# Modulation sums shared by VectorE, ScalarE and GpSimd, and held back in two stages of a two-block transformer kernel

## The chip, the cores and the metric

The kernel runs on one core of one Trainium2 chip. A core has five engines that run their own instruction streams and wait for each other through semaphores: TensorE (matmuls, in the profile PE, its weight loads PEld), VectorE (DVE), ScalarE (ACT), GpSimd (POOL) and SyncE (SP), whose queue issues the DMAs here. The metric is the device time of one execution in microseconds; lower is better.

## What is computed

Two small diffusion-transformer blocks with two layers each work on 256 latent tokens and 256 context tokens of width 1024, all in float32. The part that the change touches is the modulation: for each of four layers two condition vectors (`c` for the latent tokens, `c_ctx` for the context) are multiplied by a matrix of 1024 x 6144, which gives six rows of scales, shifts and gates per condition.

```python
def _modulation(cond, w, b):
    m = jax.nn.silu(cond) @ w + b
    return jnp.split(m[:, None, :], 6, axis=-1)

# first block, per layer
ml = _modulation(c, ada_w[i], ada_b[i])
mc = _modulation(c_ctx[None, :], ada_w[i], ada_b[i])
hl = _modulate(x, ml[0], ml[1])
yl, yc = mixer(hl, hc, ...)          # layer 0: mLSTM, layer 1: MLA attention
x = _layer_norm(ALPHA * x + ml[2] * yl, ln_g[i, 0], ln_b[i, 0])
f = _conv_ffn(_modulate(x, ml[3], ml[4]), ...)
x = _layer_norm(ALPHA * x + ml[5] * f, ln_g[i, 1], ln_b[i, 1])
```

Layer 1 of each block keeps only the latent tokens after its mixer, so the later parts of its modulation are needed for one condition alone. The second block has the same modulation around a set of parallel mixers and an MLP.

## The kernel before

Activations lie transposed: 1024 features are eight tiles of 128 partitions, and the free dimension holds the 512 tokens (256 where only the latent ones are left). A projection takes a 128-column block of weights (512 KB) at a time. `weight` loads it into one of five `raw` buffers, ScalarE casts it to a rounded high part `wh` (L280), and the low part `wl`, raw minus high, is a subtraction (L281) of which every third goes to GpSimd and the others to VectorE. `mm3` then makes three matmuls per 128x128 tile (L286 to L288): high x high, high x low, low x high. A weight takes 24 matmuls, of 512 columns in the first layer and of 256 where only the latent half is worked on. The low parts of activations are VectorE's as well (L264).

The modulation is a generator, `ada`, that runs in the background. One step loads one 128x1024 piece of its matrix into a `raw` buffer and adds it, scaled by the condition's 128 values, to an accumulator of 128x1024 per condition: the first of eight steps is a scaling on ScalarE (L418), the other seven are one VectorE instruction each (L420). After the eighth step matmuls with a column of ones add up the partitions on TensorE (tile `pa`, L427), and small operations write the result to `mod` (L439). `ada(1)` and `ada(3)` use two conditions for their first two parts and one for the rest; `ada(0)`, of which four parts run in the background, and `ada(2)` use two everywhere.

`later` queues a generator with a rate; each `weight` calls `tick`, which adds the rate times the weight's size to a credit and makes one step for each whole credit. `finish` runs a generator to its end where its result is needed. So the steps lie between the weights of whatever stage follows: `ada(0)` over the mLSTM layer's `w_up`, `w_og`, gates and head projections, `ada(1)` and the start of `ada(2)` over the first FFN, the rest of `ada(2)` over the MLA layer and the start of the second FFN, `ada(3)` over the first MLP.

The order of all instructions on each engine is settled ahead of the run by a scheduler that works from priorities and its own estimate of times; on the chip each engine runs its list in that order. A norm ends each mixer and FFN: sums of the residual and its square on VectorE and GpSimd (L509, L513, L516), eleven small VectorE operations on 128x2 or 128x4 elements that depend on each other (L525, L343, L344, L322 to L328, L352), transposes on TensorE (L336), and then the normalised tiles (L921, L922).

## Time and profile before

| | |
|---|---|
| median of 3 runs | 2603.92 us (2596.65 to 2606.05) |
| profiled execution, its own time | 2603.71 us |
| span of the profile | 2601.8 us |
| TensorE busy | 2421.3 us, 93% |
| VectorE busy | 1660.9 us, 64% |
| ScalarE busy | 1128.3 us, 43% |
| GpSimd busy | 672.7 us, 26% |
| moved by DMA | 369.69 MB, mean 142 GB/s |

The profile is one execution, and its span is 1.9 us shorter than the time measured around it. Stages follow each other in the order of the program, so a window of the span is a stage: the mLSTM layer up to about 712 us, the first FFN to 1137, the MLA layer to 1365, the second FFN to 1595, then the second block. Busy shares of the whole span mix stages with different limits; the windows say more.

### The profile page before, as it was taken

Reading aid. Unit: us, or ns where it says so; the run is one execution under the profiler, and the core shown is the slowest. Engines: PE = TensorE matmul, PEld = TensorE weight load, DVE = VectorE, ACT = ScalarE, POOL = GpSimd, SP = SyncE. Lnnn points to the kernel's source line nnn. Section 1 sums busy time; section 2 is a strip of 40 time slices with the busy share of each in tenths; the row PEclk is TensorE's granted clock in tenths of the full one; section 3 lists DMA queues with packets and bytes.
Section 4 is the critical chain, followed back from the end, with each engine's and each line's share of the span. In section 5 each row is a group of like instructions: output and inputs, shape, how many; then the busy total and the mean of one; then the engine's idle time right before and its main releaser. Section 6 shows DMA issues by size and latency. Waiting matters only on the chain.

```text
span 2601.8 us, 36381 instructions
## 1 busy us (share of the span) xinstructions
PE 2421.3 (93%) x14038; PEld 2091.6 (80%) x14038; DVE 1660.9 (64%) x2656; ACT 1128.3 (43%) x1897; POOL 672.7 (26%) x449
## 2 busy tenths in 40 slices
PE   7998999999998999997885999978999999987998
PEld 5876888788897888886675899857888878977998
DVE  4866634433666755568888756797776555597665
ACT  4733334322434233335444445765533223475543
POOL 1111322312541111154023222261211112252222
PEclk9999999999998999998997999988999999997999
DMA  8565423433422555445344655121345545223553
GB/s 288 193 208 174 146 82 113 125 102 114 144 94 90 187 173 174 155 132 160 99 142 161 202 181 175 53 84 51 125 151 171 174 158 177 67 83 109 167 176 128
DMA packets 114749, 369.69 MB, mean 142 GB/s; under 512 B 12688, under 2 KB 17040, under 8 KB 114576
## 3 DMA queue, kind: packets, MB, share of 16 engines
q1 hardware_dynamic: 114576, 367.37, 43.5%
q8 instruction: 110, 1.80, 0.3%
q14 instruction: 63, 0.52, 0.1%
HBM read 357.88 MB, written 9.44 MB: 141 GB/s over the span
## 4 chain that ended last, share of the span: by engine, by line
PE 75%; DVE 13%; DMA 4%; ACT 3%; issue 3%; POOL 1%; SPq 0%; DVEq 0%; ACTq 0%; POOLq 0%
PE pm L286 20%; PE pm L288 20%; PE pm L287 20%; PE px L286 3%; PE px L287 3%; PE px L288 3%; DVE a L420 3%; DVE wl L281 2%; DMA raw<-in_ada 2%; DVE a L1408 1%; DVE a L264 1%; PE pa L427 1%; PE px L312 1%; ACT wh L280 1%; DVE a L281 1%
## 5 line engine op out<-in xcount | busy, mean ns | idle before, releaser
L286 PE MATMUL pm<-a,wh 128*128 128x512 f32 (+1 forms) x2432 | 844.5, 349 | 17.7 <-ACT wh L280 5.8
L288 PE MATMUL pm<-a,wl 128*128 128x512 f32 (+1 forms) x2432 | 840.2, 347 | 14.3 <-DVE wl L281 12.0
L287 PE MATMUL pm<-a,wh 128*128 128x512 f32 (+1 forms) x2432 | 841.8, 347 | 0.0
L280 ACT CAST wh<-raw 128x1024 fp32r<-128x1024 f32 (+2 forms) x421 | 420.3, 1001 | 749.0 <-PE pm L287 397.0
L281 POOL TENSOR_TENSOR wl<-raw,wh 128x1024 fp32r<-128x1024 f32 (+2 forms) x140 | 334.9, 2392 | 1432.1 <-ACT wh L280 1356.7
L286 PEld LDWEIGHTS pm<-a,wh 128*128 128x128 f32 x2432 | 468.6, 193 | 90.8 <-ACT wh L280 16.7
L288 PEld LDWEIGHTS pm<-a,wl 128*128 128x128 f32 x2432 | 468.2, 193 | 72.4 <-DVE wl L281 15.0
L287 PEld LDWEIGHTS pm<-a,wh 128*128 128x128 f32 x2432 | 469.7, 193 | 53.1 <-issue 1.6
L281 DVE TENSOR_TENSOR wl<-raw,wh 128x1024 fp32r<-128x1024 f32 (+2 forms) x281 | 345.3, 1231 | 199.1 <-ACT wh L280 197.3
L420 DVE SCALAR_TENSOR_TENSOR a<-raw,cs,a 128x1024 f32<-128x1024 f32 x252 | 365.0, 1471 | 140.4 <-DMA raw<-in_ada 137.6
L287 PE MATMUL pm<-a,a 128*128 128x256 f32 (+2 forms) x844 | 252.2, 301 | 10.6 <-DVE a L264 9.7
L286 PE MATMUL pm<-a,a 128*128 128x256 f32 (+2 forms) x844 | 248.6, 306 | 14.3 <-ACT a L280 3.6
L288 PE MATMUL pm<-a,a 128*128 128x256 f32 (+2 forms) x844 | 250.4, 300 | 1.9 <-DVE a L281 1.8
L286 PEld LDWEIGHTS pm<-a,a 128*128 128x128 f32 x844 | 167.3, 202 | 21.8 <-ACT a L263 5.6
L287 PEld LDWEIGHTS pm<-a,a 128*128 128x128 f32 x844 | 169.3, 201 | 15.3 <-DVE a L264 11.6
L288 PEld LDWEIGHTS pm<-a,a 128*128 128x128 f32 x844 | 168.9, 201 | 5.1 <-DVE a L281 2.9
L263 ACT CAST a<-t 128x256 fp32r<-128x256 f32 (+2 forms) x173 | 86.4, 507 | 158.9 <-DVE t L1712 96.7
L491 DVE SCALAR_TENSOR_TENSOR a<-pm,mod,a 128x256 f32<-128x256 f32 x188 | 87.0, 479 | 101.6 <-PE pm L288 101.1
L287 PE MATMUL pm<-wl,a 128*128 128x512 f32 (+1 forms) x336 | 131.1, 390 | 5.1 <-DVE wl L281 5.1
L264 DVE TENSOR_TENSOR a<-t,a 128x256 fp32r<-128x256 f32 (+2 forms) x173 | 110.0, 642 | 36.7 <-ACT a L263 34.6
L286 PE MATMUL pm<-wh,a 128*128 128x512 f32 (+1 forms) x336 | 129.1, 387 | 3.4 <-ACT a L263 3.4
L288 PE MATMUL pm<-wh,a 128*128 128x512 f32 (+1 forms) x336 | 128.4, 390 | 0.0
(308 smaller groups left out, 3416.3 us busy)
## 6 DMA issues: line engine op xcount, KB each, us to landing
raw<-in_ada SPq DMA_DIRECT2D x192, 512.0 KB, 4.2
raw<-in_w_m SPq DMA_DIRECT2D x128, 512.0 KB, 4.0
raw<-in_ffn_in SPq DMA_DIRECT2D x88, 512.0 KB, 4.1
raw<-in_w_qk SPq DMA_DIRECT2D x32, 512.0 KB, 3.6
raw<-in_w_v SPq DMA_DIRECT2D x32, 512.0 KB, 3.5
raw<-in_ffn_oa SPq DMA_DIRECT2D x32, 512.0 KB, 4.1
raw<-in_w_inb SPq DMA_DIRECT2D x28, 512.0 KB, 4.2
raw<-in_w_up SPq DMA_DIRECT2D x16, 512.0 KB, 4.8
```

The costliest lines, as they stand in the source:

```text
L263: self.nc.scalar.copy(hi, src)
L264: self.nc.vector.tensor_sub(lo, src, hi.bitcast(F32))
L280: nc.scalar.copy(hi, raw)
L281: eng.tensor_sub(lo, raw, hi.bitcast(F32))
L286: mm(out, ah, bh, start=start, stop=False)
L287: mm(out, ah, bl, start=False, stop=False)
L288: mm(out, al, bh, start=False, stop=stop)
L312: self.nc.tensor.matmul(out_ps[:, i * nt + t:i * nt + t + 1], a[:, c0 + t * P:c0 + (t + 1) * P], self.ones[:, 0:1], start=(k == 0), stop=( ...
L420: nc.vector.scalar_tensor_tensor(s, raw, c, s, op0=ALU.mult, op1=ALU.add)
L427: nc.tensor.matmul(ps[32 * i:32 * i + 32], self.ones[:, 0:32], acc[i // 2][:, 512 * (i % 2):512 * (i % 2) + 512], start=True, stop=True, t ...
L491: self.nc.vector.scalar_tensor_tensor(z[:, a:b], ps[:, a:b], gate[:, kt, w:w + 1], z[:, a:b], op0=ALU.mult, op1=ALU.add)
L1408: nc.vector.scalar_tensor_tensor(y3, x(i), w(i), y3, op0=ALU.mult, op1=ALU.add)
```

## The change

In a part with two conditions, the first condition's accumulator stays VectorE's. The second one's piece is scaled by ScalarE into a new tile, from the same pool of 31 tiles that holds activations, and GpSimd adds that tile to the accumulator. A part with one condition stays on VectorE. `pause` runs the steps of a part that has been begun to the part's end and then stops all steps until `hold` is reset; it is called ahead of the mLSTM heads and ahead of the MLA layer. The rates become 0.9 for `ada(0)` (from 0.8), 1.1 for `ada(1)` (from 0.8), 1.1 for `ada(2)` (from 1.2), and 0.6 for what is left of `ada(2)` after the MLA layer.

```diff
                     if kt == 0:
                         nc.scalar.activation(s, raw, AF.Copy, scale=c)
+                    elif s is acc[0]:
+                        nc.vector.scalar_tensor_tensor(s, raw, c, s, op0=ALU.mult, op1=ALU.add)
                     else:
-                        nc.vector.scalar_tensor_tensor(s, raw, c, s, op0=ALU.mult, op1=ALU.add)
+                        x = self.a4(F32, (P, D))
+                        nc.scalar.activation(x, raw, AF.Copy, scale=c)
+                        nc.gpsimd.tensor_add(s, s, x)
+                self.open = True
                 if kt < KD - 1:
                     yield
+            self.open = False
...
     def tick(self, size):
-        if not self.bg:
+        if not self.bg or self.hold:
             return
...
+    def pause(self):
+
+        while self.open:
+            next(self.bg[0][0])
+        self.hold = True
...
-    K.later(rest, 0.8)
+    K.later(rest, 0.9)
...
+    K.pause()
     qps = [qk_of(0)]
...
         y += head_out(hd, vp, pp)
+    K.hold = False
...
-        K.later(gen1, 0.8)
+        K.later(gen1, 1.1)
...
-        K.later(gen2, 1.2)
+        K.later(gen2, 1.1)
...
+        K.pause()
         _mla(K, h1, z, mod1, _Ln(K, z, g2, b2, K.affine(mod1, 4, 3, g2, b2), ALPHA, h, LAT, LAT))
+        K.hold = False
+        K.bg[0][1] = 0.6
```

In the program's order of loads, the first FFN has 54 modulation steps before and 72 after, the MLA layer 27 and none, the second FFN 15 and 24; the head projections have about ten before and none after, and `w_mo` gets 8.

VectorE at the norm that ends the MLA layer, before: `v` and `rs` are the norm's small tiles, the `a` tiles with `cs` the modulation's accumulators.

```order
L343 SCALAR_TENSOR_TENSOR v_10996<-st_10994 128x2
L420 SCALAR_TENSOR_TENSOR a_10957<-raw_11160,cs,a_10957 128x1024
L420 SCALAR_TENSOR_TENSOR a_10958<-raw_11160,cs,a_10958 128x1024
L344 SCALAR_TENSOR_TENSOR v_10996<-v_10996,st_10994 128x2
L420 SCALAR_TENSOR_TENSOR a_10957<-raw_11170,cs,a_10957 128x1024
L420 SCALAR_TENSOR_TENSOR a_10958<-raw_11170,cs,a_10958 128x1024
L322 TENSOR_SCALAR rs_10999<-v_10996 128x2
L420 SCALAR_TENSOR_TENSOR a_10957<-raw_11239,cs,a_10957 128x1024
L420 SCALAR_TENSOR_TENSOR a_10958<-raw_11239,cs,a_10958 128x1024
L323 TENSOR_TENSOR rs_10999<-rs_10999 128x2
```

The same place of the changed program, where the lines are numbered one and up to fifteen higher.

```order
L538 TENSOR_SCALAR st_11065<-px_11052 128x4
L344 SCALAR_TENSOR_TENSOR v_11067<-st_11065 128x2
L345 SCALAR_TENSOR_TENSOR v_11067<-v_11067,st_11065 128x2
L323 TENSOR_SCALAR rs_11070<-v_11067 128x2
L324 TENSOR_TENSOR rs_11070<-rs_11070 128x2
L325 SCALAR_TENSOR_TENSOR rs_11070<-rs_11070,v_11067 128x2
```

The modulation's accumulations are gone from between the norm's steps; they stand behind the norm in the changed order.

GpSimd at the first weights of the second FFN, before: the norm's last scalings (`ga`), then the low parts of every third weight.

```order
L927 TENSOR_SCALAR a_4945<-a_4945,ga_9193 128x256 x2
L281 TENSOR_TENSOR wl_11238<-raw_11235,wh_11237 128x1024
L281 TENSOR_TENSOR wl_11342<-raw_11339,wh_11341 128x1024
L281 TENSOR_TENSOR wl_11493<-raw_11490,wh_11492 128x1024
L281 TENSOR_TENSOR wl_11596<-raw_11593,wh_11595 128x1024
```

And in the changed program, where L425 is the new addition.

```order
L942 TENSOR_SCALAR a_4939<-a_4939,ga_9438 128x256 x2
L282 TENSOR_TENSOR wl_11301<-raw_11298,wh_11300 128x1024
L425 TENSOR_TENSOR a_11156<-a_11156,a_11234 128x1024
L425 TENSOR_TENSOR a_11156<-a_11156,a_11305 128x1024
L282 TENSOR_TENSOR wl_11389<-raw_11386,wh_11388 128x1024
L425 TENSOR_TENSOR a_11156<-a_11156,a_11381 128x1024
L425 TENSOR_TENSOR a_11156<-a_11156,a_11458 128x1024
L282 TENSOR_TENSOR wl_11536<-raw_11533,wh_11535 128x1024
```

Between two low parts of weights GpSimd now has one or two additions.

## Rows read from the trace of the kernel before

**Rows 1.** The page's first part: busy time by engine, share, instructions.

```profile
PE 2421.3 (93%) x14038; PEld 2091.6 (80%) x14038; DVE 1660.9 (64%) x2656; ACT 1128.3 (43%) x1897; POOL 672.7 (26%) x449
```

**Rows 2.** Windows by stage: length, busy time of each engine, clock, DMA share, GB/s.

```profile
257.00:405.00 148.00, 147.16 (x699) 122.11 (x699) 69.39 (x104) 54.70 (x102) 42.41 (x41) 1.00 0.37 117
620.00:712.00 92.00, 90.81 (x423) 75.30 (x422) 50.77 (x81) 36.94 (x50) 36.20 (x18) 1.00 0.39 127
712.00:850.00 138.00, 127.64 (x872) 117.90 (x871) 86.10 (x154) 54.60 (x94) 44.60 (x45) 0.94 0.32 106
850.00:1000.00 150.00, 150.00 (x667) 121.16 (x666) 93.73 (x104) 49.70 (x61) 23.26 (x9) 1.00 0.52 171
1137.00:1180.00 43.00, 35.17 (x249) 32.97 (x247) 34.73 (x71) 17.84 (x36) 28.90 (x24) 0.87 0.42 126
1180.00:1365.00 185.00, 156.47 (x958) 133.63 (x958) 159.07 (x293) 87.78 (x178) 44.83 (x26) 0.94 0.43 135
1365.00:1404.00 39.00, 16.03 (x98) 12.78 (x97) 31.71 (x54) 12.92 (x28) 16.25 (x15) 0.65 0.41 136
1404.00:1450.00 46.00, 37.56 (x274) 35.76 (x274) 42.94 (x48) 23.48 (x34) 9.80 (x4) 0.93 0.65 210
1450.00:1595.00 145.00, 143.49 (x1183) 141.26 (x1180) 88.59 (x145) 75.28 (x117) 39.45 (x17) 1.00 0.56 176
```

**Rows 3.** The chain of work from 1180 to 1365, shares by line.

```profile
by line: DVE a L420 19.8%; issue 9.1%; PE pm L287 8.4%; PE pm L286 8.3%; PE pm L288 8.1%; DVE a L264 7.7%; DMA raw<-in_ada 5.4%; PE px L286 4.1%; PE px L287 3.6%; DVE wl L281 3.4%; PE px L288 3.3%; PE pa L427 2.6%; PE pm L1150 2.4%; DVE a L
```

**Rows 4.** Windows again, L420 alone: length, VectorE busy, clock, DMA.

```profile
1180.00:1365.00 185.00, 58.95 (x44) 0.94 0.43 135
```

**Rows 5.** VectorE in order of time, 1352 to 1395: start, length, what.

```profile
1371.55 0.15 DVE L525 TENSOR_SCALAR st<-px 128x4 f32<-128x4 f32 x1
...
1379.60 2.47 DVE L420 SCALAR_TENSOR_TENSOR a<-raw,cs,a 128x1024 f32<-128x1024 f32 x2
...
1385.52 2.48 DVE L420 SCALAR_TENSOR_TENSOR a<-raw,cs,a 128x1024 f32<-128x1024 f32 x2 [0.72 <-DMA raw<-in_ada]
...
1388.50 0.16 DVE L352 TENSOR_TENSOR st<-st,rs 128x2 f32<-128x2 f32 x1
```

**Rows 6.** Waits of the whole span: us in total, times, longest.

```profile
PE pa L427 <- DVE a L420: 29.3, 5, 20.4
```

**Rows 7.** Lines 418 and 420: duration in ns, least, median, most.

```profile
L418 ACT ACTIVATE a<-raw,cs x36: 1129/1148/1220, 94.2 to 2161.1; 128x1024 f32<-128x1024 f32 x36
L420 DVE SCALAR_TENSOR_TENSOR a<-raw,cs,a x252: 1260/1280/3433, 95.8 to 2176.0; 128x1024 f32<-128x1024 f32 x126
```

**Rows 8.** Groups by shape, 1450 to 1595: busy us, mean ns, idle before.

```profile
L281 POOL TENSOR_TENSOR wl<-raw,wh 128x1024 fp32r<-128x1024 f32 x15 | 36.1, 2405 | 99.0 <-ACT wh L280 99.0
L365 DVE SCALAR_TENSOR_TENSOR t<-pm,pv,t 128x255 f32<-128x255 f32 x16 | 7.6, 478 | 3.9 <-ACT t L362 3.8
L1074 DVE TENSOR_TENSOR t<-t,pm 128x256 f32<-128x256 f32 x16 | 6.6, 417 | 4.9 <-ACT t L1073 4.2 <-PE pm L288 0.7
```

**Rows 9.** Groups by shape, 850 to 1000, VectorE.

```profile
L420 DVE SCALAR_TENSOR_TENSOR a<-raw,cs,a 128x1024 f32<-128x1024 f32 x23 | 33.7, 1476 | 28.1 <-DMA raw<-in_ada 28.0
L281 DVE TENSOR_TENSOR wl<-raw,wh 128x1024 fp32r<-128x1024 f32 x18 | 21.9, 1219 | 4.3 <-ACT wh L280 4.0
...
L365 DVE SCALAR_TENSOR_TENSOR t<-pm,pv,t 128x510 f32<-128x510 f32 x10 | 7.4, 741 | 4.3 <-ACT t L362 4.3
L1074 DVE TENSOR_TENSOR t<-t,pm 128x512 f32<-128x512 f32 x10 | 6.8, 684 | 11.9 <-PE pm L288 10.4 <-ACT t L1073 1.5
```

**Rows 10.** VectorE and GpSimd in order of time, at 139 and 699.

```profile
139.36 4.61 DVE L420 SCALAR_TENSOR_TENSOR a<-raw,cs,a 128x1024 f32<-128x1024 f32 x2
140.18 2.71 POOL L281 TENSOR_TENSOR wl<-raw,wh 128x1024 fp32r<-128x1024 f32 x1 [13.96 <-ACT wh L280]
...
699.63 6.41 POOL L281 TENSOR_TENSOR a<-raw,a 128x1024 fp32r<-128x1024 f32 x1 [5.23 <-ACT a L280]
701.42 2.35 DVE L281 TENSOR_TENSOR a<-raw,a 128x1024 fp32r<-128x1024 f32 x2
```

More of the change, by code (lines that the diff above doesn't have):

```diff
@@ L199, in __init__ @@
         self.credit = 0.0
+        self.hold = self.open = False
         cp = self.cp
```

## The prediction, made before the change was run

> **What bounds the kernel now.** I read the page's first part first: TensorE is busy 93% of the span, VectorE 64%, ScalarE 43%, GpSimd 26% [rows 1]. So the gain can only be TensorE's idle time, and the time it works at the low clock. Next I cut the span into stages [rows 2]: the row of a stage shows how long it is, how much of it TensorE was busy, and the granted clock. The stages that wait are easy to see. The mLSTM stages do not: of 148 us at the head projections TensorE is busy 147.2, at w_mo 90.8 of 92, in the middle of the first FFN 150 of 150. The losses that touch this change stand in four rows: the end of the first FFN's last norm (1137 to 1180, 35.2 of 43), the MLA layer (1180 to 1365, 156.5 of 185, clock 0.94), the norm that ends it (1365 to 1404, 16.0 of 39, clock 0.65) and the first weights of the second FFN (1404 to 1450, 37.6 of 46). From 1450 on no modulation step is left, and TensorE is busy 143.5 of 145 us.
>
> What ends the waits there is the chain's to say: in the MLA layer 19.8% of it is L420, the modulation sum on VectorE, 5.4% the landing of its weights and 2.6% its last matmuls on TensorE [rows 3]. L420 is busy for 59 of the 185 us, and VectorE as a whole for 159 [rows 2, 4]. At the norm the reader sees the worst case in order of time: the statistics arrive at 1371.55, the last small operation of the chain ends at 1388.66, and between the tiny steps, 0.15 us each, stand pairs of L420 of some 2.5 us [rows 5]. TensorE meanwhile stands in its queue before the modulation's own matmul, 20.4 us at once [rows 6].
>
> **The change, part by part.** Two-condition parts of the modulation have 98 accumulations for their second condition (7 of each 8 steps, in 4, 2, 6 and 2 parts). These leave VectorE, at 1.28 us each undisturbed, and become 98 scalings on ScalarE, for which the nearest row is L418 at 1.15 us, and 98 additions on GpSimd. The nearest row to these is its 128x1024 subtraction, 2.41 us in an undisturbed stretch [rows 7, 8]. 98 times 1.28 is 125 us off VectorE, 113 more on ScalarE, 236 more on GpSimd. None of this is on TensorE; all counts only where it makes a weight late.
>
> *Heads.* Ten or so steps leave the head projections; the row shows 0.8 us of idle time to win there, so 0. They come back as 8 steps at w_mo, where VectorE is busy for 51 of 92 us and the 8 steps bring it 9 us: 0. In the gate stage and the og projections I see gains and losses of 2 to 3 us each way; the sum for all mLSTM stages and for the MLP, whose rate stays, is +1, from -5 to +8.
>
> *MLA layer.* All 27 steps leave it. TensorE idles 28.5 of the 185 us, and 6% of 156.5, 9.4 us, is what the clock took: 38 us is the upper bound. If every wait on L420 is replaced by the next wait of the layer's own (chains of norm, softmax and split stay on VectorE, 100 us of the 185), a third is left, 12 us. I take 28, because the modulation's shares of the chain add up to 27.8% of 185, 51 us, more than all that is idle. From 1137 to 1180 I take 3. With the step goes its DMA: SP's queue carries no modulation load between w_dkv and the second FFN, so nothing is moved past a waiting load there.
>
> *The norm after it.* Rows of the changed order show its eleven small operations back to back. At 0.15 us these are 1.7 us where now 17.1 pass [rows 5]: -15, and 2 more for the clock, which was granted at 0.65 around it: -17, between -8 (other waits take over) and -22.
>
> *Second FFN.* Here the bill comes. 24 steps at 0.6 per weight lie on the first 40 weights, where before 15 lay near its start. In the clean stretch 24 matmuls of a weight take 24 x 145/1183 = 2.94 us [rows 2]. Per weight two thirds of a VectorE subtraction (1.22) and a third of one on GpSimd (2.41) are there already [rows 8, 9], and half a hidden split (0.21, taken as half the 0.42 of the product of the same size). The change adds 0.6 x 7/8 = 0.525 accumulations on VectorE (0.67 us) and 0.525 additions on GpSimd (1.26 us).
>
> Now the one question that decides the size: do these run side by side? The trace says no. At 139.36 two L420 take 4.61 us instead of 2.5, the second ending about a microsecond after the GpSimd subtraction (140.18 to 142.89) that it met; at 699.63 a GpSimd subtraction takes 6.41 us, and VectorE's own subtractions run one behind the other until 703.8 before it ends, some 2.3 us later [rows 10]. Operations that read two operands of SBUF on both engines take turns. So their times add up: 0.81 + 0.80 + 0.21 + 0.67 + 1.26 = 3.75 us a weight, over 2.94. That is 0.81 x 40 = 32 us. Below it the bound is 0, if weights loaded ahead cover it; above it VectorE stands still for every GpSimd operation and does its PSUM work (0.69 us a weight: two tap operations and a product for two weights, [rows 8]) on top: 4.44 us, 60 us. I take 32. Before, the start lost 46 - 274 x 0.1226 = 12.4 us, which goes away as such: net +20, from -12 to +48. Five raw buffers are no tighter than this: 1.6 loads in 3.75 us are 224 GB/s, and 210 GB/s were moved from 1404 to 1450 [rows 2].
>
> The Trainium skill (SBUF — State Buffer, "SBUF: two separate sides") calls the ports that VectorE and GpSimd share an exclusive lock, held for the whole instruction, and not a split of bandwidth; the trace agrees, 4.61 us for 2.5. It speaks against handing additions to GpSimd at all. Without the split, the same 24 steps would cost VectorE 0.81 + 0.21 + 0.69 + 1.34 = 3.05 us a weight and the pair 3.16, so +9 in place of +32, and a sum 23 us lower.
>
> *First FFN.* 72 steps in place of 54, of which 40 have two conditions. Its start (712 to 850) has the same disturbed norm as above, mildly: TensorE idles 10.4 us. One L420 of each pair is gone there: -6 (0 to -10). Where two-condition steps run at 1.1 per weight, over some 36 weights, the same sum is 0.81 + 0.80 + 0.34 (half a product of 0.68, [rows 9]) + 0.96 x (1.28 + 2.41) = 5.49 us, against 24 x 150/667 = 5.40 on TensorE: +3; I take +6 for imperfect packing. Upper bound: plus the taps and product, (2 x 0.74 + 0.68) / 2 = 1.08 [rows 9], so 6.57 and +42.
>
> **Sum.** -3 - 28 - 17 + 20 - 6 + 6 + 1 = -27 us against the profiled execution's own 2603.7 (span 2601.8 and 1.9 outside it), which is the median shown (2603.92) but for 0.2: 2577.
>
> **Rivals.** *A, the forecast*: 2577; with the MLA term and the second FFN's each off by some 10 us, 2558 to 2596. The holds remove more than the denser FFNs cost.
>
> *B, slower: VectorE stands for each GpSimd addition*, in the FFNs, so that the weights' second parts come late. Price: the upper bounds, +48 in the second FFN and +42 in the first; -48 - 6 + 48 + 42 + 1 = +37, so 2641. It decides from about 4.0 us a weight in the second FFN if the first loses 30 as well. For it: the second L420 at 139.36. By the lock that the Trainium skill states (above) this is the case in which VectorE always comes second. Against it: in 850 to 1000 L420 takes 1.48 us in the mean, so it is held up like that there too, and TensorE never waits [rows 2, 9].
>
> *C, same: the layer's own waits take over* in the MLA, as in the lower bounds: -3 - 12 - 10 + 20 + 0 + 1 = -4, so 2600. For it: VectorE works 100 us there without L420, in short dependent steps.
>
> *D, much faster: the second FFN hides its steps*, because weights stand ready ahead and GpSimd's third of the weights has slack: that term is -10 and the first FFN's 0: -48 - 10 - 6 + 0 + 1 = -63, so 2541.
>
> That the change doesn't do what it says can be excluded: the order shows no modulation row in the heads and the MLA.
>
> **How the numbers follow.** A 0.48, C 0.20, D 0.17, B 0.15. The forecast is A's. The range leaves about one in ten on each side: D's far half below 2545, most of B above 2622. About 0.5%, 13 us, is what a measurement of this kernel can tell from no change, so faster means below 2591: most of A (0.43), all of D, a little of C (0.03): 0.63. Same: the rest of A (0.05), most of C: 0.20. Slower: B and a tail of C: 0.17.
>
> **What the next profile would show.** Right: no L421 between 1137 and 1390 or so; the norm's small operations back to back and TensorE's gap there under 8 us; clock near 1.0 in the MLA. In the first 40 weights of the second FFN TensorE busy below 85%, VectorE's 128x1024 subtraction and accumulation well above 1.3 us in the mean, GpSimd's addition near 2.5 us, and the time from first to last of them near 150 us for 40 weights. Wrong: if that stretch takes 118 us (D) or 178 (B), or if the MLA layer keeps more than 170 of its 185 us (C). A further way to be wrong is a TensorE wait on the second sum's matmul, which now hangs on GpSimd, the slowest of the three; the order puts it one to four weights behind the first sum's, and I count nothing for it.

## The result, and the profile of the changed kernel

The changed kernel takes 2640.57 us (median of 4, 2638.10 to 2643.18) against 2603.02 us for the kernel before (4 runs, 2596.65 to 2606.05). The ratio is 1.0148, with a 95% interval from 1.0124 to 1.0171: slower by 38 us, where 27 us faster was forecast. The profiled execution of after took 2638.37 us, with a span of 2636.6 us, 34.8 more than before. Lines below the edit are numbered differently: L420 of before is L421, L418 is L419, L280 and L281 are L281 and L282, L427 is L434; the new scaling is L424 and the new GpSimd addition L425.

The page's first part, to be read beside [rows 1]:

```profile
PE 2442.4 (93%) x14038; PEld 2105.2 (80%) x14038; DVE 1671.4 (63%) x2558; ACT 1231.5 (47%) x1997; POOL 927.6 (35%) x547
```

VectorE lost 98 instructions, as intended, and is 10.5 us *busier* than before. The groups by shape over the whole span show why (after the bar: busy us, mean ns of one):

```profile
L282 DVE TENSOR_TENSOR wl<-raw,wh 128x1024 fp32r<-128x1024 f32 x245 | 364.4, 1490 | 244.5 <-ACT wh L281 243.2
...
L425 POOL TENSOR_TENSOR a<-a,a 128x1024 f32<-128x1024 f32 x98 | 274.1, 2798 | 264.5 <-ACT a L424 251.8 <-PE pm L289 6.5 <-PE pm L288 4.3
L421 DVE SCALAR_TENSOR_TENSOR a<-raw,cs,a 128x1024 f32<-128x1024 f32 x154 | 267.2, 1735 | 145.4 <-DMA raw<-in_ada 139.9 <-ACT a L419 4.6
```

The same two VectorE groups of before:

```profile
L420 DVE SCALAR_TENSOR_TENSOR a<-raw,cs,a 128x1024 f32<-128x1024 f32 x252 | 365.0, 1471 | 140.4 <-DMA raw<-in_ada 137.6 <-ACT a L418 2.5
L281 DVE TENSOR_TENSOR wl<-raw,wh 128x1024 fp32r<-128x1024 f32 x245 | 315.2, 1289 | 197.6 <-ACT wh L280 196.1
```

The accumulation went from 1.47 to 1.74 us in the mean (1.28 is its median in before [rows 7]), the weights' subtraction from 1.29 to 1.49 (1.22 undisturbed [rows 9]), and the GpSimd addition takes 2.80 against the 2.41 that was taken for it. An operation's recorded length contains the time in which it stands, that is, in which it counts as busy and makes no progress.

Next, the windows by stage, moved to where the same weights now lie (columns as in [rows 2]):

```profile
628.00:721.00 93.00, 91.35 (x425) 75.47 (x424) 61.66 (x80) 40.39 (x53) 40.20 (x21) 1.00 0.42 138
721.00:781.00 60.00, 55.14 (x421) 52.03 (x420) 38.19 (x63) 20.71 (x39) 39.90 (x37) 0.94 0.25 86
...
879.00:1029.00 150.00, 150.00 (x663) 118.80 (x662) 96.67 (x108) 54.94 (x66) 29.49 (x12) 1.00 0.59 202
...
1225.00:1371.00 146.00, 138.71 (x926) 126.24 (x925) 108.88 (x238) 80.95 (x171) 36.21 (x26) 0.98 0.27 84
1371.00:1391.00 20.00, 13.58 (x83) 12.68 (x82) 16.41 (x40) 13.10 (x26) 10.87 (x15) 0.68 0.26 87
1391.00:1438.00 47.00, 37.55 (x269) 35.62 (x270) 39.55 (x37) 27.73 (x39) 30.27 (x11) 0.89 0.60 205
1438.00:1545.00 107.00, 90.25 (x652) 83.17 (x650) 89.47 (x82) 57.58 (x74) 62.31 (x22) 0.90 0.60 202
1545.00:1620.00 75.00, 69.77 (x550) 67.41 (x551) 50.60 (x83) 37.74 (x63) 20.49 (x9) 0.98 0.48 156
```

The MLA layer came down from 185 to 146 us at a clock of 0.98, and TensorE idles 7.3 us in it, where it idled 28.5. The middle of the first FFN is as full as before. The second FFN is now the stage that waits: from 1391 to 1545 TensorE is busy 127.8 of 154 us, and the granted clock is 0.89 to 0.90.

Both kernels run the same 14038 matmuls, so the end of each stage can be matched by its last weight's last matmul. Worked out in this way, for after and for the runs told below, in us longer (+) or shorter than in the profile of before (mLSTM from w_up to w_mo; first FFN; MLA; the norm after it; second FFN; mixers; MLP). The rows below the first are experiments 3, 6, 16, 4, 8, 12 and 13 in this order:

```
                              mLSTM  FFN 1    MLA   norm  FFN 2  mixers   MLP    sum
after                         +19.6  +25.1  -38.5  -19.0  +37.7    -3.1  +12.9  +34.7
additions on VectorE           +0.1  +11.4  -43.1  -19.0  +23.1    -0.2   +0.2  -27.5
memsets for additions          +0.4   +2.2  -39.6  -19.0   +6.1    -2.8   +0.3  -52.2
two additions on VectorE       +4.8  +32.8  -40.0  -19.0  +42.1    -2.2   +2.7  +21.1
MLA hold alone                 +0.3   +8.8  -42.7  -17.9  +12.8    +1.1   -0.6  -38.3
all steps in first FFN         -1.5  +39.5  -44.2  -19.9  -15.4    -1.1    0.0  -42.6
the same, low parts VectorE    -7.7  +31.6  -42.4  -18.3  -18.7    +2.0   -6.2  -59.6
after, low parts VectorE      +10.7  +21.8  -44.6  -18.7  +28.5    +2.5   +4.4   +4.6
```

Each row is one execution. That of experiment 6 is some 11 us shorter than its other three, so its row is too low by about as much.

The w_mo stage is the plainest place to see the mechanism. VectorE and then GpSimd in order of time, from 714, of after (start, length, line, how many in a row):

```profile
714.92 3.43 DVE L421 SCALAR_TENSOR_TENSOR a<-raw,cs,a 128x1024 f32<-128x1024 f32 x1
718.27 5.67 DVE L265 TENSOR_TENSOR a<-a,a 128x512 fp32r<-128x512 f32 x2
723.87 0.86 DVE L504 SCALAR_TENSOR_TENSOR a<-pm,mod,a 128x256 f32<-128x256 f32 x2
724.65 9.20 DVE L282 TENSOR_TENSOR a<-raw,a 128x1024 fp32r<-128x1024 f32 x3
...
734.57 5.98 DVE L282 TENSOR_TENSOR a<-raw,a 128x1024 fp32r<-128x1024 f32 x2
...
714.86 8.54 POOL L425 TENSOR_TENSOR a<-a,a 128x1024 f32<-128x1024 f32 x3 [13.57 <-ACT a L424]
723.35 2.81 POOL L282 TENSOR_TENSOR a<-raw,a 128x1024 fp32r<-128x1024 f32 x1
726.12 3.35 POOL L425 TENSOR_TENSOR a<-a,a 128x1024 f32<-128x1024 f32 x1
729.42 3.35 POOL L282 TENSOR_TENSOR a<-raw,a 128x1024 fp32r<-128x1024 f32 x1
732.74 3.39 POOL L425 TENSOR_TENSOR a<-a,a 128x1024 f32<-128x1024 f32 x1
```

GpSimd never stops from 714.86 to 736.13, and in that stretch each VectorE subtraction of two SBUF operands takes about as long as one GpSimd operation: 9.20 us for three, where one alone took 1.22 [rows 9]. Two 128x512 subtractions take 5.67 us; two alone took 1.29 at 712.92 in the same view. In between, VectorE's accumulations out of PSUM (L504) take their usual 0.43 each. TensorE then idles 4.9 of the 60 us from 721, at a clock of 0.94: 3.0 us behind ScalarE's casts, the first of which had waited 3.1 us for VectorE (L265), and 1.9 behind VectorE's subtraction; in before it was busy 49.0 of 49 from 712 to 761. Of the 19.6 us that the mLSTM layer lost, 8.5 are there ahead of w_mo and 11.1 come in it.

### The profile page after: what moved, and what is told of

The parts are those of the page before. It is cut to its first block, busy times and chain, and to the rows that moved or that the text cites. A ratio compares the mean times of both kernels' runs of the same rounds, so it can differ in the third digit from the quotient of the medians.

```text
span 2636.6 us, 36558 instructions
## 1 busy us (share of the span) xinstructions
PE 2442.4 (93%) x14038; PEld 2105.2 (80%) x14038; DVE 1671.4 (63%) x2558; ACT 1231.5 (47%) x1997; POOL 927.6 (35%) x547
## 5 line engine op out<-in xcount | busy, mean ns | idle before, releaser
L281 ACT CAST wh<-raw 128x1024 fp32r<-128x1024 f32 (+2 forms) x421 | 419.0, 1000 | 633.1 <-PE pm L288 308.6
L282 POOL TENSOR_TENSOR wl<-raw,wh 128x1024 fp32r<-128x1024 f32 (+2 forms) x140 | 334.5, 2389 | 1041.7 <-ACT wh L281 1002.3
L282 DVE TENSOR_TENSOR wl<-raw,wh 128x1024 fp32r<-128x1024 f32 (+2 forms) x281 | 396.1, 1413 | 250.9 <-ACT wh L281 249.1
L425 POOL TENSOR_TENSOR a<-a,a 128x1024 f32<-128x1024 f32 x98 | 274.1, 2798 | 264.5 <-ACT a L424 251.8
L421 DVE SCALAR_TENSOR_TENSOR a<-raw,cs,a 128x1024 f32<-128x1024 f32 x154 | 267.2, 1735 | 145.4 <-DMA raw<-in_ada 139.9
L287 PE MATMUL pm<-a,a 128*128 128x256 f32 (+2 forms) x844 | 256.2, 311 | 18.0 <-ACT a L281 8.3
L289 PE MATMUL pm<-a,a 128*128 128x256 f32 (+2 forms) x844 | 255.0, 305 | 13.7 <-DVE a L282 13.7
L288 PE MATMUL pm<-a,a 128*128 128x256 f32 (+2 forms) x844 | 257.4, 307 | 5.9 <-DVE a L265 4.8
L287 PEld LDWEIGHTS pm<-a,a 128*128 128x128 f32 x844 | 173.2, 207 | 27.9 <-ACT a L281 10.6
L289 PEld LDWEIGHTS pm<-a,a 128*128 128x128 f32 x844 | 172.7, 205 | 19.3 <-DVE a L282 15.5
L288 PEld LDWEIGHTS pm<-a,a 128*128 128x128 f32 x844 | 173.7, 206 | 10.4 <-DVE a L265 6.6
L265 DVE TENSOR_TENSOR a<-t,a 128x256 fp32r<-128x256 f32 (+2 forms) x173 | 121.8, 710 | 39.2 <-ACT a L264 35.4
L504 DVE SCALAR_TENSOR_TENSOR a<-pm,mod,a 128x256 f32<-128x256 f32 x188 | 86.6, 478 | 93.8 <-PE pm L289 93.6
L424 ACT ACTIVATE a<-raw,cs 128x1024 f32<-128x1024 f32 x98 | 110.1, 1146 | 71.8 <-DMA raw<-in_ada 71.7
```

Source lines behind the costliest of these rows:

```text
L265: self.nc.vector.tensor_sub(lo, src, hi.bitcast(F32))
L281: nc.scalar.copy(hi, raw)
L282: eng.tensor_sub(lo, raw, hi.bitcast(F32))
L287: mm(out, ah, bh, start=start, stop=False)
L288: mm(out, ah, bl, start=False, stop=False)
L289: mm(out, al, bh, start=False, stop=stop)
```

## The experiments

Three theories stood at the start. *Ports*: VectorE stands while GpSimd reads its operands, so the split itself costs the time. *Density*: the holds push the steps into the FFNs, and these pay. *Scaling*: the extra pass on ScalarE, with its extra tile, delays ScalarE's other work. Diffs are against after where nothing else is said. The runs were taken in several sessions, in which before itself had medians from 2603.0 to 2607.3 us, so a difference between sessions is uncertain by some 4 us.

**1. No split; the holds and rates stay.**

```diff
-                    elif s is acc[0]:
-                        nc.vector.scalar_tensor_tensor(s, raw, c, s, op0=ALU.mult, op1=ALU.add)
                     else:
-                        x = self.a4(F32, (P, D))
-                        nc.scalar.activation(x, raw, AF.Copy, scale=c)
-                        nc.gpsimd.tensor_add(s, s, x)
+                        nc.vector.scalar_tensor_tensor(s, raw, c, s, op0=ALU.mult, op1=ALU.add)
```

> The changed kernel with every accumulation back on VectorE; holds and rates as changed. Ports theory (GpSimd's additions and VectorE's two-operand work take turns, and this costs in every stage with steps, not in the second FFN alone): the second FFN's 38 us of extra time fall to about 9, the extra 11 us of the second half of w_mo, 25 of the first FFN and 11 of the MLP to a few: 2565 to 2585 us. Density theory (the steps cost because more of them lie in a stage, whoever adds): 2625 to 2650 us.

Measured: 2573.32 us, ratio to before 0.9871 (0.9853 to 0.9890). Without the split the rest of the change is worth 34 us.

**2. The split alone, in the kernel before** (the same lines the other way round; no hold, no new rate).

> The kernel before with the split alone; no holds, old rates. Ports theory: slower than before by 25 to 70 us, 2630 to 2675, since the MLA layer now has the additions too, at a place where VectorE is busy for 159 of 185 us. Density theory: within 10 us of before, 2593 to 2613.

Measured: 2640.24 us, ratio 1.0133 (1.0113 to 1.0153). That the total is the one of after is a coincidence: the split alone costs 33 us (2607.24 in that session), half of the 67 that it costs on top of the holds and rates (2640.57 less experiment 1), and with the split in place the holds and rates gain nothing. By the stages the split alone costs 19.4 us in the MLA layer, 18.7 in the norm behind it and the second FFN, and next to nothing in the mLSTM layer (+0.3), the first FFN (-0.3) and the MLP (+2.1).

**3. Scaling on ScalarE, addition on VectorE.**

```diff
-                        nc.gpsimd.tensor_add(s, s, x)
+                        nc.vector.tensor_add(s, s, x)
```

> The changed kernel, scaling still on ScalarE into the extra tile, but the addition on VectorE. Ports theory: as without the split, 2565 to 2590, for VectorE's work is the same (an addition for an accumulation) and GpSimd has none of it. Scaling theory (ScalarE's queue stands before a modulation load, or the extra tile takes a place in the pool of 31, and weights come late by that): stays above 2625. Density theory: 2625 to 2650.

Measured: 2573.35 us, ratio 0.9873 (0.9858 to 0.9889), the same as with no split. So ScalarE's 98 scalings and their tiles cost nothing that could be told, and one word, the engine of the addition, is worth 67 us. The scaling theory is out. Its page row:

```profile
PE 2422.3 (94%) x14038; PEld 2085.5 (81%) x14038; DVE 1658.4 (64%) x2656; ACT 1231.7 (48%) x1997; POOL 653.4 (25%) x449
```

VectorE does the 98 additions itself here and is 13 us *less* busy than in after, where GpSimd does them.

**4. The hold in the MLA layer and the FFN rates alone** (no split, no hold in the heads, rate 0.8 at the mLSTM's start).

```diff
-    K.pause()
     qps = [qk_of(0)]
...
-    K.hold = False
 
     for ft in range(KD):
...
-    K.later(rest, 0.9)
+    K.later(rest, 0.8)
```

> No split, no hold at the mLSTM heads and the old rate of 0.8 there; the hold at the MLA layer and the other rates as changed. Ports theory with the prediction's price of nothing for the heads: within 8 us of the run without the split, 2560 to 2590. If the 8 steps at w_mo cost in themselves, 8 to 15 us faster than that run. Density theory: 2610 to 2640.

Measured: 2565.89 us, ratio 0.9844 (0.9829 to 0.9859). The density theory is out as an account of the loss: with the hold in the MLA layer and the denser FFNs, and without the split, the kernel is 41 us faster than before in that session (2607.24). The FFNs do pay for their steps, 8.8 and 12.8 us, but less than the MLA layer and its norm give back.

**5. Half the addition.**

```diff
-                        nc.gpsimd.tensor_add(s, s, x)
+                        nc.gpsimd.tensor_add(s[:, 0:512], s[:, 0:512], x[:, 0:512])
```

> The kernel after, but each of the 98 GpSimd additions adds only the first 512 of 1024 columns (it leaves out half of the second condition's sum); instructions, waits, queue order and ScalarE's scalings stay. The 128x512 addition on GpSimd takes 1.24 us elsewhere in this program, the full one 2.80 in the profile of after. Ports theory (VectorE stands while GpSimd reads two SBUF operands, so the cost goes with GpSimd's busy time): the 67 us between after and the version with the addition on VectorE shrink to 67 x 1.24 / 2.80 = 30, so 2573 + 30 = 2603, between 2592 and 2615. Rival, a price per instruction (semaphores, the hand-over from ScalarE to GpSimd, the order in the queues): unchanged, 2630 to 2645.

Measured: 2583.18 us, ratio 0.9901 (0.9870 to 0.9933). The direction is that of the ports, but the time is below the range given: GpSimd's time on additions fell from 274.1 to 154.0 us, and the cost from 67 to 10. Experiment 17 comes back to this. A price per instruction is out, since the 98 instructions are all still there.

**6. Memsets in place of the additions.**

```diff
-                        nc.gpsimd.tensor_add(s, s, x)
+                        for _ in range(3):
+                            nc.gpsimd.memset(x, 0.0)
```

> The kernel after, but in place of each addition GpSimd writes zeros three times over the 128x1024 scaled tile (it leaves out the second condition's sum). A 128x1024 memset takes 0.95 us in the trace of before, so GpSimd is busy for 2.86 us a step, as long as the addition, and still waits for ScalarE's scaling; but it reads no operand. Ports theory: VectorE is not held up, 2573 (2565 to 2585), VectorE's 128x1024 subtraction back to some 1.35 us in the mean. Rival, GpSimd's queue (every third weight's subtraction stands behind the addition in GpSimd's program order, and TensorE waits for that weight): GpSimd is as busy as before, so 2630 to 2650, with TensorE's waits on weights that GpSimd prepares.

Measured: 2562.07 us (2551.29 to 2562.55; the profiled execution is the shortest), ratio 0.9818 (0.9787 to 0.9848). The page row, and then groups by shape over the span:

```profile
PE 2407.2 (94%) x14038; PEld 2085.6 (82%) x14038; DVE 1542.6 (61%) x2558; ACT 1230.2 (48%) x1995; POOL 911.9 (36%) x743
```

```profile
L282 DVE TENSOR_TENSOR wl<-raw,wh 128x1024 fp32r<-128x1024 f32 x245 | 322.3, 1318 | 234.4 <-ACT wh L281 232.9
...
L426 POOL MEMSET a<- 128x1024 f32 x294 | 274.1, 955 | 227.6 <-ACT a L424 222.1
...
L421 DVE SCALAR_TENSOR_TENSOR a<-raw,cs,a 128x1024 f32<-128x1024 f32 x154 | 216.3, 1404 | 189.9 <-DMA raw<-in_ada 184.6 <-ACT a L419 4.5
```

This is the cleanest pair of the study. GpSimd spends 274.1 us on memsets here and 274.1 us on additions in after, both waiting for ScalarE (222.1 and 251.8 us), with every third weight's subtraction behind them. VectorE has the same 2558 instructions. The reading of operands is gone, and VectorE is busy 1542.6 us instead of 1671.4. Gone too is what waits for the second sum, but in after only ScalarE waited for an addition on GpSimd, twice, 4.3 us in all; TensorE, whose wait for it the prediction named as a danger, has none. So GpSimd's queue is not the cause, and the standing is measured: 128.8 us, 1.31 us for each addition of 2.80. By the Trainium skill (SBUF — State Buffer, "Who interferes with whom") a VectorE instruction with two inputs in SBUF contends with a GpSimd instruction that reads SBUF and not with one that only writes it; this pair of runs agrees.

**7. The hold in the heads, added to experiment 4.**

```diff
+    K.pause()
     qps = [qk_of(0)]
...
         y += head_out(hd, vp, pp)
+    K.hold = False
```

> The version with the MLA hold alone (2565.9) plus the hold during the mLSTM heads, its rate at the mLSTM's start still 0.8. Theory: the hold in the heads removes nothing (TensorE idles 0.8 us there) and packs 8 steps onto w_mo, so it costs most of the 7 us by which the version without the split but with both holds (2573.3) is behind: 2570 to 2574. Rival: it is the rate 0.9 at the start of the mLSTM stages that costs them: 2564 to 2568.

Measured: 2567.64 us, ratio 0.9846 (0.9820 to 0.9872): within 2 us of experiment 4, in the range that the rival gave. The hold in the heads does nothing to the time that could be told. Whether the rate 0.9 costs the 7 us between experiments 1 and 4 stays open, since the intervals of experiments 1 and 7 overlap. By the stages the mLSTM layer isn't longer with it (-2.4 us in experiment 1, +0.3 in 4); the second FFN is, +26.7 against +12.8 with the same 38 accumulations in it, and no run shows why.

**8. All 96 steps in the first FFN** (against experiment 4).

```diff
-        K.later(gen1, 1.1)
+        K.later(gen1, 1.45)
...
-        K.later(gen2, 1.1)
+        K.later(gen2, 1.45)
...
-        K.bg[0][1] = 0.6
```

> The version with the MLA hold alone (2565.9), but both rates in the first FFN are 1.45 in place of 1.1, so that all 96 steps end there and none is left for the second FFN. The second FFN then gives back what its steps cost: 13 us over before and some of the 12 that before lost there itself. Theory (VectorE and GpSimd take turns): at 1.45 a two-condition weight needs 0.81 + 0.80 + 0.34 + 1.08 + 1.45 x 0.875 x 2 x 1.28 = 6.3 us against 5.40 on TensorE, +25 over some 28 weights at most, and one-condition weights fit: between 2545 and 2575, 2560 the likeliest. Rival (weights wait for their loads: 2.45 loads of 0.5 MB in 5.4 us are 238 GB/s, more than any stretch of before moved): the first FFN stretches by over 30 us, 2580 or more.

Measured: 2560.26 us, ratio 0.9821 (0.9794 to 0.9847), in the range expected. The parts were not: by the stages the first FFN is 39.5 us longer than before, more than the theory's 25 and past the rival's 30, and the second 15.4 shorter; experiment 4 had +8.8 and +12.8. In the middle of the first FFN the loads kept up: from 850 to 1000 the trace has 208 GB/s with TensorE busy 150 of 150 us.

**9. The middle: rates 1.25, 1.25, then 0.3** (against experiment 4).

```diff
-        K.later(gen1, 1.1)
+        K.later(gen1, 1.25)
...
-        K.later(gen2, 1.1)
+        K.later(gen2, 1.25)
...
-        K.bg[0][1] = 0.6
+        K.bg[0][1] = 0.3
```

> The version with the MLA hold alone (2565.9; rates 1.1, 1.1, then 0.6), with the rates 1.25, 1.25, then 0.3: 82 of 96 steps in the first FFN. With 1.45 and none later it took 2560.3: by its trace the first FFN was 38 us longer than in before and the second 15 us shorter. If the cost of a step rises steadily with the rate, 1.25 lies between the two, 2560 to 2566. If the first FFN has slack up to some rate (its one-condition stretch lost nothing at 1.45) and the second at 0.3 has it too, it is below both: 2545 to 2558.

Measured: 2568.18 us, ratio 0.9860 (0.9839 to 0.9881), a little above both expectations. No gain shows at the rate between; by the stages 13 us of it lie in the MLA layer's gain, -29.2 in place of -42.7.

**10 and 11. The split in one half of the program alone.** First only beside the mLSTM stages and the MLP, then only beside the FFNs.

```diff
-                    elif s is acc[0]:
+                    elif s is acc[0] or l in (1, 2):
```

> The kernel after, but with the split only for the modulations that run beside the mLSTM stages and the MLP (42 of 98 additions on GpSimd; the other 56 accumulations on VectorE). The prediction priced the change in these stages at +1: 2573 + 1 = 2574. By the stages of the two traces (after less the version with the additions on VectorE: up projection +6, og +8, w_mo +6, MLP +9, w_qk -1) the same split costs 27 there: 2600, between 2590 and 2608.

```diff
-                    elif s is acc[0]:
+                    elif s is acc[0] or l in (0, 3):
```

> The reverse: the split only for the modulations that run beside the two FFNs (56 of 98 additions on GpSimd). The prediction priced the split in the second FFN at 23 us (+32 in place of +9) and in the first at 0 to 6: 2573 + 23 to 29 = 2596 to 2602. By the stages of the two traces (first FFN +14, the MLA's first weights +4, second FFN +15): 2606, between 2598 and 2615. If the two halves add up, this one's cost and that of the split beside mLSTM and MLP make 67; if VectorE's queue carries lateness from stage to stage, they make less.

Measured: 2598.46 us, ratio 0.9975 (0.9961 to 0.9990), and 2604.82 us, ratio 0.9998 (0.9979 to 1.0018). Against 2573 without GpSimd's additions that is 25 and 31 us. The prediction priced the first at 1 and the second at 23 to 29. So the sum of the split's cost in the FFNs came near what was foreseen, by luck: after less experiment 3 has 14 us of it in the first FFN (0 to 6 foreseen) and 15 in the second (23 foreseen). That beside the mLSTM and the MLP was not foreseen at all. They add up to 56 of 67; where the other 11 arise is not shown.

**12. Every low part on VectorE** (against experiment 8): GpSimd reads nothing for weights or modulation any more.

```diff
-        eng = nc.gpsimd if self.wtoggle % 3 == 0 else nc.vector
+        eng = nc.vector
```

> The version with all 96 steps in the first FFN (2560.3; no additions on GpSimd), but VectorE makes the low part of every weight, where GpSimd made each third (135 subtractions of mostly 128x1024, 2.49 us each on GpSimd, 1.28 on VectorE). It asks whether GpSimd is worth its port at all. If VectorE stands for all of GpSimd's time, moving a subtraction over gains 1.2 us of it, and the dense stretch of the first FFN some 11 us: 2545 to 2556. If it stands for about half (128.8 us over 98 additions of 2.80 us between the profile of after and that of the version with memsets, 1.31 us each), the two are worth the same, 2556 to 2566. If GpSimd's third ran beside VectorE for nothing, VectorE's 150 us more cost: 2580 or more.

Measured: 2536.85 us, ratio 0.9746 (0.9721 to 0.9771), the fastest version of the study, 2.5% below before and below the best expectation. VectorE does 162 more subtractions (2818 instructions against 2656) and is busy 1685.1 us, only 25 more than in experiment 8 (1660.2), because its own operations became shorter. Windows of the second FFN, and groups by shape:

```profile
1330.00:1376.00 46.00, 36.34 (x258) 34.30 (x257) 34.84 (x72) 28.20 (x54) 14.62 (x19) 0.85 0.39 129
1376.00:1521.00 145.00, 145.00 (x1211) 145.00 (x1210) 99.56 (x161) 76.84 (x117) 0.00 (x0) 1.00 0.59 183
```

```profile
L282 DVE TENSOR_TENSOR wl<-raw,wh 128x1024 fp32r<-128x1024 f32 x367 | 456.2, 1246 | 309.1 <-ACT wh L281 301.6 <-PE pm L289 5.2 <-issue 0.3
L421 DVE SCALAR_TENSOR_TENSOR a<-raw,cs,a 128x1024 f32<-128x1024 f32 x252 | 318.6, 1292 | 93.4 <-DMA raw<-in_ada 90.0 <-ACT a L419 2.5
```

From 1376 on TensorE is busy 145.0 of 145 us, with VectorE at 69% and GpSimd at nothing; no step is left in the second FFN. In before it was 143.5 of 145 [rows 2].

**13 to 15. The same move in after, in before and in experiment 4.** The diff is that of experiment 12 each time.

> The kernel after (the split kept: 98 additions on GpSimd), but VectorE makes the low part of every weight. The same move brought 23 us to the version without a split (2560.3 to 2536.9). If the additions cost by themselves (1.31 us of VectorE for each), their 67 us stay: 2640 - 23 = 2617, 2600 to 2630. If they cost only in company (an addition and a weight's subtraction one behind the other on GpSimd hold both a second of VectorE's work and the weight), most of the 67 us go: 2550 to 2580.

> The kernel before with VectorE making the low part of every weight: nothing of the change. If the move brings the same everywhere, 2604 - 23 = 2581, 2574 to 2588; VectorE's 128x1024 subtraction and accumulation at about 1.25 and 1.29 us as in the version measured. If it brings more where modulation steps stand in the MLA layer (there VectorE is the bound), down to 2560. If VectorE's 7% of added work counts in the MLA and the norms, where its queue is long already, 2600 or more.

> The version with the MLA hold alone (2565.9; rates 1.1, 1.1, then 0.6) with VectorE making the low part of every weight. If the move brings the same everywhere, 2543; the version with the rates 1.45 and none later had 2536.9. If the 0.6 in the second FFN fits now (a weight there needs 1.22 + 0.21 + 0.69 + 0.6 x 0.875 x 2 x 1.28 = 3.5 us of VectorE against 2.94 on TensorE, nothing on GpSimd), it is not better: 2540 to 2550. If the slack of weights loaded ahead covers it, 2530 to 2537.

Measured: after with it 2604.51 us, ratio 0.9987 (0.9971 to 1.0003); before with it 2580.67 us, ratio 0.9900 (0.9865 to 0.9934); experiment 4 with it 2546.33 us, ratio 0.9759 (0.9726 to 0.9793). Each lies in a range that was named, 13 and 14 in the first and 15 in the second. The move brings 20 to 26 us to the three versions without the split and 36 to after. So 58 us lie between after and experiment 4 in this form too (2604.51 less 2546.33), against 75 without the move; both contain the 7 us between experiments 1 and 4. Most of the split's cost comes from the additions by themselves, and a smaller part from their meeting GpSimd's subtractions.

**16 and 17. Where the standing falls, and how long one hold is.** The first is experiment 3 with a second, idle addition on VectorE; the second cuts GpSimd's addition in two.

```diff
-                        nc.gpsimd.tensor_add(s, s, x)
+                        nc.vector.tensor_add(s, s, x)
+                        nc.vector.tensor_add(x, x, x)
```

> The version with scaling on ScalarE and addition on VectorE (2573.4), with a second 128x1024 addition of two operands on VectorE behind each of the 98 (it doubles the scaled tile, which nobody reads any more). VectorE then spends about 2 x 1.18 = 2.4 us for each step's second condition, as long as GpSimd's addition in the kernel after. If the time that one engine after the other takes for its two-operand work is what counts (98 x 2.4 us, whoever does it), it is as slow as the kernel after: 2625 to 2650. If VectorE's own work falls where it can wait, and the standing does not, it stays far below: 2580 to 2605.

```diff
-                        nc.gpsimd.tensor_add(s, s, x)
+                        for i in (0, 512):
+                            nc.gpsimd.tensor_add(s[:, i:i + 512], s[:, i:i + 512], x[:, i:i + 512])
```

> The kernel after, with each GpSimd addition cut into two of 128x512 (1.24 us each elsewhere in this program, so GpSimd is busy for some 2.5 to 3.1 us a step as before). If the length of one hold matters (VectorE's short operations of the norms and the PSUM reads behind it stand for the whole of it), the cost falls by a third or more: 2590 to 2620. If only the sum of the holds counts, 2630 to 2655.

Measured: 2624.60 us, ratio 1.0081 (1.0060 to 1.0101), and 2623.98 us, ratio 1.0076 (1.0059 to 1.0092). The first comes out just under the "who does it doesn't matter" case: the row of its page

```profile
PE 2437.2 (93%) x14038; PEld 2098.6 (80%) x14038; DVE 1783.1 (68%) x2754; ACT 1232.3 (47%) x1997; POOL 685.4 (26%) x449
```

shows VectorE 124.7 us busier than in experiment 3, and the time is 51 us longer. The step from experiment 6 to experiment 3, 115.8 us of additions, had cost 11. So VectorE's time is cheap up to about experiment 3 and dear beyond it. By the stages some 40 us of the step lie in the two FFNs; that the slack of these dense stages is used up would explain it, and is not shown. That the time comes near after's is partly chance: beside the mLSTM, the mixers and the MLP experiment 16 loses 5.3 us, where after loses 29.4, and in the FFNs 74.9 against 62.8. VectorE's own work does not stand in for GpSimd's everywhere.

The second lies between its two ranges. It lowers the cost by 17 of 67 us although GpSimd is busy longer (333.4 us with additions in place of 274.1). Its page has

```profile
PE 2443.2 (93%) x14038; PEld 2093.9 (80%) x14038; DVE 1630.4 (62%) x2558; ACT 1231.9 (47%) x1997; POOL 980.5 (37%) x645
```

and with VectorE's busy time above experiment 6 as a measure of its standing (2558 instructions in each), the shorter operations make VectorE stand less in sum, 87.8 us in place of 128.8. Experiment 5 falls in with this: VectorE is busy 1585.0 us there, which is 42.4 of standing. Against experiment 6 the three cost 21, 62 and 78 us for 42, 88 and 129 us of standing, 0.5 to 0.7 us for each. So the cost follows VectorE's standing more nearly than GpSimd's busy time, and that the length of one hold counts beyond that is not shown.

## Why the prediction was wrong

**The step that failed** is the pricing of the split outside the second FFN: "the sum for all mLSTM stages and for the MLP, whose rate stays, is +1", with "w_mo, where VectorE is busy for 51 of 92 us and the 8 steps bring it 9 us: 0", and the first FFN at "I take +6". The first was measured at +29.4 with the mixers (+19.6, -3.1 and +12.9), the second, start and end together, at +25.1 against -3. That is 56 of the 62 us between the forecast of -27 and the span's +34.7; the second FFN was 18 us dearer than forecast, and the MLA layer and its norm gave 12 more. Not all of the 56 is the split: without GpSimd's additions (experiment 3) the first three come to +0.1, but the first FFN still to +11.4. So of the 25.1 us there 13.7 are the split's, and 11.4 the steps' with every sum on VectorE. The exclusive use of the shared operands had been read correctly out of [rows 10], and was then applied to the second FFN alone; elsewhere VectorE's free time in a window was taken as cover. The rows at 714 show what that overlooks. VectorE was busy 61.7 of 93 us from 628 to 721 and 38.2 of 60 behind it, with a third of either window free, but the additions come in a row on GpSimd, and each of VectorE's subtractions then takes as long as one of them, with TensorE waiting for what they hold up. Experiment 10 sizes this at 25 us, and experiment 6 shows that it is the reading of operands. It takes the denser steps as well: with the split at the old places and rates (experiment 2) the mLSTM layer is 0.3 us longer than before. Whether the rate 0.9 or the hold in the heads makes the difference, and why the MLP, whose rate is the same in all, loses 12.9 us in after and 2.1 in experiment 2, no run shows.

**MLA layer and norm**: the direction was right, the sizes low. The layer saved 38.5 us, the end of the interval given (28 taken, -12 to -38), and 43.1 without GpSimd's additions. The norm after it saved 19.0 against 17, partly by luck: its eleven operations were put at 0.15 us each, 1.7 us, and take 4.0, so the chain gave 13 of the 19 us and not 15, and the rest gave 6 and not 2. VectorE's norm chain in after runs back to back, to be read beside [rows 5]:

```profile
1372.38 0.16 DVE L538 TENSOR_SCALAR st<-px 128x4 f32<-128x4 f32 x1
...
1375.44 0.70 DVE L329 SCALAR_TENSOR_TENSOR rs<-rs 128x2 f32<-128x2 f32 x1
1376.17 0.16 DVE L353 TENSOR_TENSOR st<-st,rs 128x2 f32<-128x2 f32 x1
```

That is 4.0 us where 17.1 passed. TensorE idles 6.4 of the 20 us around it, under the 8 that were named. No L421 stands from 1225 to 1371.

**Second FFN**: VectorE's standing is there as foreseen, the size was low, and part of the cost has another source. Groups by shape of after, 1391 to 1545:

```profile
L425 POOL TENSOR_TENSOR a<-a,a 128x1024 f32<-128x1024 f32 x20 | 57.1, 2859 | 42.2 <-ACT a L424 41.9
L282 DVE TENSOR_TENSOR wl<-raw,wh 128x1024 fp32r<-128x1024 f32 x26 | 54.4, 2102 | 7.8 <-ACT wh L281 7.8
...
L421 DVE SCALAR_TENSOR_TENSOR a<-raw,cs,a 128x1024 f32<-128x1024 f32 x19 | 43.0, 2261 | 9.8 <-DMA raw<-in_ada 9.8
...
L282 POOL TENSOR_TENSOR wl<-raw,wh 128x1024 fp32r<-128x1024 f32 x13 | 35.9, 2765 | 20.8 <-ACT wh L281 18.0 <-ACT a L424 2.9
...
L265 DVE TENSOR_TENSOR a<-t,a 128x256 fp32r<-128x256 f32 x15 | 13.8, 926 | 3.3 <-ACT a L264 3.2
```

VectorE's three kinds of two-operand work stand 26 x 0.88 + 19 x 0.98 + 15 x 0.52 = 49 us here (against 1.22, 1.28 and the 0.41 that L265 takes in the clean end of the norm). TensorE ran 921 matmuls in these 154 us by the two windows above, worth 112.9 at the clean rate, and lost 7.6 us more until 1620: 48.7 us gross where 32 were forecast, +37.7 net where +20 was. 154 us for 921 / 24 = 38.4 weights are 4.0 us a weight, between the 3.75 taken and the 4.44 of the upper bound, which had VectorE's PSUM work "on top"; that this work makes the difference is not shown. The price of the steps without the split, put at +9 gross, was the larger error: with the same steps experiment 3 pays +23.1 net, 35.5 gross, and experiment 4 +12.8 net, 25.2 gross. So the 23 us named for the split in this stage are 15 by the one and 25 by the other, and the steps themselves are dear there even on VectorE alone; with next to no GpSimd instruction in its way (experiment 15) the stage still pays 11.8.

**Rival B** gave 2641 and the time is 2640.57, but by sums that partly cancel: it had the FFNs 10 and 8 us too dear (+48, and +33 with start and end; 37.7 and 25.1 measured), +1 for the mLSTM stages and the MLP, where 29.4 fell, and saved 12.5 too little in the MLA and the norm. So the number is luck. Its mechanism, VectorE standing for GpSimd's additions, is what experiments 3, 5 and 6 show. Its place, "in the FFNs", is half of it. The evidence held against it, that from 850 to 1000 TensorE never waits, was true and stayed true (150.0 of 150 from 879 to 1029): there nearly all steps have one condition, and GpSimd makes 3 of its 98 additions.

**What stays open**: why a microsecond of standing costs more than one of VectorE's own work (128.8 us of standing cost 78 us, after against experiment 6, while experiment 16 pays 62 for 240.5 us of own additions). By the stages the difference lies beside the mLSTM, the mixers and the MLP, where experiment 16 loses 5.3 us in all; what makes it was not separated.

## What to carry to other kernels

Moving work from VectorE to GpSimd did not relieve VectorE here, because GpSimd reads its two operands from SBUF while VectorE does the same; writing alone did not disturb it. Compare VectorE's busy time and the mean length of its *unchanged* operations before and after, not its instruction count. When a background task is moved out of a stage that waits, ask what it costs in every stage that receives it, also in those that show no idle time now; cover is not a window's average but what is free when the next weight is due. And try the plain move in the other direction: taking GpSimd's old share of such work back to VectorE was worth 20 to 36 us in the four versions tried, more than the tuning of rates.

## What the runs showed of the hardware

A GpSimd memset of the same length in time adds nothing to VectorE's two main operations (subtraction and accumulation 1.318 and 1.404 us in the mean, against 1.305 and 1.416 in experiment 3), where an addition of two operands makes it stand 1.31 us for every 2.80. With GpSimd's subtractions for the weights gone too, the same two operations take 1.246 and 1.292 us (experiment 12). VectorE's standing is recorded inside its instructions as busy time, so 63% busy in after hides some 129 us in which it did nothing. It goes both ways: GpSimd's addition, 2.41 us where it came first, at 1471.51 in the trace of after, took 2.80 in the mean and 3.46 at most. Standing did not reach operations that take one of their two tensors from PSUM: L504 has a mean of 0.48 us in before (as L491) and in after, and the first tap operation of the FFN (L365, in after L366) 0.74 us in both for its 128x510 shape.
